# Issue order at the start, layer-1 modulation pieces on VectorE, and a fixed order of adds at both layer ends of a two-layer diffusion trunk

## The chip, the cores and the metric

The kernel runs on one core of a Trainium2 chip. The metric is the device time of one execution in microseconds (us), the median of three runs. Below, PE (TensorE), VectorE (DVE), ScalarE (ACT), GpSimd (POOL) and SyncE (SP) are the engines of that core. Matmul inputs come from on-chip memory (tiles); matmul results land in accumulator banks (PSUM).

## What is computed

Two trunk layers over 512 latent tokens and 256 context tokens, of width 1024, all in fp32. Layer 0 mixes tokens with windowed attention, layer 1 with a chunked gMLP. After each mixer there is a LayerNorm, then a mixture of experts (16 experts, two per token, one router for both layers), then a second LayerNorm. Shift, scale and gate of each step come from a "modulation" product of the conditioning vector.

```
mod = silu(c) @ w_mod[i] + b_mod[i]           # shift, scale, gate; 6 x 1024 per layer
x   = layer_norm(ALPHA * x + g_a * mixer(x * (1 + sc_a) + sh_a))
y   = sum over 2 experts e of gate_e * (silu(h @ w1[e]) * (h @ w3[e])) @ w2[e]
x   = layer_norm(ALPHA * x + g_f * y)         # "layer end" below
# gMLP: z = gelu(h @ w_in + b_in); u, v = halves of z
#       v = layer_norm(v); s = w_s (per group of 128 channels) @ v + b_s; out = (u * s) @ w_out
```

## The kernel before, in words

**Weights as pieces.** All weights stream from HBM as pieces of 128 x 1024 fp32 (512 KB). The list `pieces` (L153 to 185) fixes in which order they are loaded, and `issue` (L194) starts them on the SP queue, each into a tile of the pool `S`, which has 28 tiles (`NS`, L25). That pool is shared with split weights, intermediates and the rows that come back from the experts, so a load waits until a tile is free. `raw`, `hl` and `adv` (L248 to 262) start loads ahead: `LR` and `LS` say how many pieces ahead to load and to split, and inside the experts `LOOK` = 25 does (L1159). `split` (L226) turns a piece into a high and a low part, a ScalarE cast and a VectorE subtraction, for the matrices that go through three matmuls instead of one.

**The start (L266 to 430).** SP loads a block of columns, the first modulation pieces (`mod`), two blocks of constants (`ct`, `cc`), two small rows of 16 numbers (`sinkv`, `rb`) that are broadcast to 128 partitions, and writes zeros to the rows of the HBM array `ydr` that stand for "no result". 16 `mod` pieces go through PE (`gemv`, L336); their result `mcol` modulates the context (`cT`) and the tokens (`xT`) in `hsplit` (L402), which yields a high and a low part on ScalarE and VectorE. With the split `qkv` pieces these feed the first projection (L439 to 441).

**Modulation pieces on vectors.** The other 80 modulation pieces (`mt`; 32 of layer 0, 48 of layer 1) are multiplied by the row silu(c) and summed along the row, in `gemt` (L365): either in one VectorE instruction (L368), or as a GpSimd product (L370) and a ScalarE sum (L371). 64 of them run beside the attention. The last 16 run beside the gMLP, two in each of its 8 steps, odd ones on VectorE, even ones on GpSimd and ScalarE. For these 16 the row silu(c) is loaded again just ahead of the 8 steps (L1402).

**Experts (`moe`, L1126).** Tokens are gathered from HBM into units of 32, 64 or 128 rows. 12 pieces per expert pass through `gemm1` (L1045) and `gemm2` (L1078). Most units write their result to `ydr` by a GpSimd DMA; the last two units stay in PSUM. `collect` (L1111) gathers the two results of each token back from `ydr` with 8 indirect GpSimd DMAs, and `combine` (L1120) adds each to the token's row with one VectorE instruction.

**Layer end (`last_norm`, L681).** The last two units are spread to their tokens by matmuls with a 0/1 matrix (`rows`, L692) into PSUM, VectorE adds that to `X` (`add`, L701), ScalarE sums squares (L710), and VectorE computes 1/sqrt by Newton steps on tiny tiles (`newton`, L737) for two token tiles at a time. In layer 0, `pre` (L1334) then transposes the normalised rows for the gMLP, and GpSimd multiplies and adds the LayerNorm row (L1355, L1356). In layer 1 each tile is normalised on ScalarE (L1439), multiplied (L1440) and added to (L1441) on VectorE, but for the first two tiles whose addition is on GpSimd, and stored.

**gMLP.** `vhalf` (L1359) makes v in 8 steps of 24 matmuls; `vnorm` (L1367) normalises each of the four token tiles; then 8 steps (L1404 to 1429) each make one 128-channel block of u (24 matmuls, L1409 to 1411), mix v (L1419), and multiply on VectorE (L1422, L1425, L1428).

**What sets the order.** The build orders each engine's instructions with a simulated timeline (L1497): of those whose inputs it expects to be there, the one written first goes first, and `high_priority` blocks go ahead. `in_order` (L667) ties the instructions of a block on the named engines to the order in which they are written. Before, `last_norm` uses it for its own additions and norms, while `combine` stands outside it.

Of the kernel before, what the change touches and what calls it, by code (L numbers as in the profile page):

```python
# [18 lines left out]
D = 1024  # L19
# [85 lines left out]
def hybrid_kernel(ctx: ExitStack, tc: tile.TileContext, A, out):  # L105
# [127 lines left out]
    def ensure_split(n):  # L233
        while nsplit[0] < min(n, limit[0]):
            p = pieces[nsplit[0]]
            if p[0] not in KSPLIT:
                if p[0] == "zero":
                    issue(nsplit[0] + 1)
                elif nsplit[0] not in used:
                    return  # L240
            else:
                issue(nsplit[0] + 1)
                pairs[p] = split(raws[p])
            nsplit[0] += 1
# [164 lines left out]
    cT, hT = {}, {}  # L409
    att = ExitStack()  # L410
# [270 lines left out]
    def last_norm(l, X, py, gf):  # L681
# [5 lines left out]
        v = [small([128, 3, 2], F32, "xv") for _ in range(2)]  # L687
        o = [psA(), psA(), psT(), psT()]
        o = [[o[0][:, :512], o[0][:, 512:]], [o[1][:, :512], o[1][:, 512:]], o[2:], [psB(), psB()]]
        ys = slot([128, 512], F32, "ys")  # L690

        def rows(t, u, y):  # L692

            for n in range(2):
                PE.matmul(o[t][n], R["oT"][n * 64:n * 64 + 64, u, t * 128:(t + 1) * 128], y[n * 64:n * 64 + 64, :],
                          start=(u == 0), stop=(u == 1))

        for t in range(4):
            rows(t, 0, R["yp"])
# [13 lines left out]
        def var(t):  # L713
            w = v[t // 2][:, 0, t % 2:t % 2 + 1]
# [3 lines left out]
        def norm(i):  # L718
            var(2 * i)
            var(2 * i + 1)  # L720
            y = newton([v[i][:, k] for k in range(3)], "x", 2)
            nmr = small([128, 2], F32, "xm")
            V.tensor_mul(nmr, nmu[:, 2 * i:2 * i + 2], y)
            return y, nmr

        with in_order(PE, V, SC):
            V.scalar_tensor_tensor(ys, py, R["gs"][:, 1:2], gf, op0=OP.mult, op1=OP.mult)
            for t in range(4):
                rows(t, 1, ys)
            for t in range(4):  # L730
                add(t, 0)
                add(t, 1)
                mean(t)
            r = norm(0), norm(1)
        return r

    def newton(v, w, n=1):  # L737

        y = small([128, n], F32, w + "ny")
# [5 lines left out]
        u = small([128, n], F32, w + "nu")  # L745
# [374 lines left out]
    def combine(l, a, X):  # L1120

        R = RT[l]
        for t in range(4):
            V.scalar_tensor_tensor(X[t], R["y", t, a], R["g"][:, a, t:t + 1], X[t], op0=OP.mult, op1=OP.add)  # L1124

    def moe(l, rest, X):  # L1126
# [25 lines left out]
        def stage(i):  # L1152
# [3 lines left out]
            def adv():  # L1156
                if lastuse:
                    done[0] += 1
                    issue(first + done[0] + LOOK)  # L1159
            return lambda j: raw("moe", l, v, j), adv  # L1160

        def fin():
# [4 lines left out]
            elif i == n - 2:  # L1167
                R["yp"] = slot([128, 512], F32, "ys")
                V.scalar_tensor_tensor(R["yp"], py, R["gs"][:, 0:1], gf[64], op0=OP.mult, op1=OP.mult)
            return py  # L1170

        for i, (v, o, m, row) in enumerate(units):
# [17 lines left out]
            if i == n // 2:  # L1190
                gates()
            if i == n - 4:
# [6 lines left out]
            if i == n - 1:  # L1199
                combine(l, 1, X)  # L1200
            pend = (i, to_hT(m, s))
        py = fin()
        combine(l, 0, X)
# [113 lines left out]
    binv = load_row(A["binv"], alloc=uslot)  # L1317

# [48 lines left out]
    def vnorm(t):  # L1367
        v = vv[t]
        rstd, nmr = ln_stats(v, "c")
        SC.activation(v, v, AF.Identity, bias=nmr, scale=rstd)  # L1370

    for t, (y, nmr) in zip((0, 2), last_norm(0, X, py, gf)):
        for i in range(2):
            SC.activation(X[t + i], X[t + i], AF.Identity, bias=nmr[:, i:i + 1], scale=y[:, i:i + 1])
# [13 lines left out]
    for t in range(4):  # L1388
        vhalf(t, 1)
        vnorm(t)  # L1390
# [11 lines left out]
    srow[0] = load_row(sdr, alloc=uslot)  # L1402
    gated = []
    for f in range(8):  # L1404
# [7 lines left out]
        for j in range(2):  # L1412
            gemt(1, 32 + 2 * f + j)
# [22 lines left out]
    for t, (y, nmr) in zip((0, 2), last_norm(1, X, py, gf)):  # L1436
        for i in range(2):
# [63 lines left out]
```

## Time and profile before

| | |
|---|---|
| three runs, us | 1185.77, 1188.14 (median), 1191.42 |
| the profiled execution, us | 1186.24 |
| its span, first to last instruction | 1184.4 |
| mean granted PE clock | 0.925 |
| busy: PE, VectorE, ScalarE, GpSimd | 1014.6, 611.5, 359.9, 271.2 us |
| DMA | 330.62 MB, mean 279 GB/s |

The span runs through start (to about 86 us), attention (to 290), layer 0's output projection and router (to 380), layer 0's experts (to 647), layer end (to 674), gMLP (to 860, with its output projection and router), layer 1's experts (from 886 to 1147), layer end. Shares are means over these stages, so each stage is read on its own below. "Busy" counts time inside instructions; a PE clock of 1.00 is 2.4 GHz and 0.50 is 1.2 GHz.

### The profile page before, as it was taken

The page shows a single profiled execution, that of the slowest core. Times are in us where ns is not written, and L with a number is a line of the kernel's source. Part 1 is how long each engine was busy: PE and PEld are TensorE (multiplying, and loading weights), DVE is VectorE, ACT ScalarE, POOL GpSimd, SP SyncE. Part 2 cuts the span into 40 slices and gives each one's busy share as a digit, 9 for nine tenths or more (in the row PEclk, how much of TensorE's full clock was granted, in tenths as well). Part 3 has the DMA queues.
Part 4 walks back from the last instruction along what each step waited for, and adds up shares of the span by engine and source line. Part 5 has one row for each costly group of instructions (what it writes and reads, how often), then busy time and mean ns, then how long its engine had stood idle before and what let it go on. Part 6 is the DMA issues. An engine that isn't in the chain of part 4 may idle for free. (4 is left out here: it accounts for less than half of the span.)

```text
span 1184.4 us, 18461 instructions
## 1 busy us (share of the span) xinstructions
PE 1014.6 (86%) x6596; PEld 589.6 (50%) x6596; DVE 611.5 (52%) x1548; ACT 359.9 (30%) x730; POOL 271.2 (23%) x262
## 2 busy tenths in 40 slices
PE   5799899996992999999999399599929999999980
PEld 2577665554782444444443178488713342444420
DVE  1798988785457621221122896876565121221247
ACT  1553487775312111111121343442212110111103
POOL 0044333323000123231213251410001221120131
PEclk7799999998996999999999799799959999999995
DMA  9934457547274999999998316365449999898991
GB/s 346 408 148 174 157 196 258 173 145 256 102 269 160 377 409 390 410 410 409 410 386 324 118 46 244 131 212 203 178 189 387 410 411 410 311 407 352 386 382 71
DMA packets 104284, 330.62 MB, mean 279 GB/s; under 512 B 13346, under 2 KB 24306, under 8 KB 104179
## 3 DMA queue, kind: packets, MB, share of 16 engines
q1 hardware_dynamic: 88608, 287.56, 63.4%
q0 software_dynamic: 10848, 26.75, 6.0%
q10 hardware_dynamic: 4722, 14.98, 3.5%
q8 instruction: 56, 0.92, 0.3%
q14 instruction: 50, 0.40, 0.1%
HBM read 310.72 MB, written 21.67 MB: 281 GB/s over the span
## 5 line engine op out<-in xcount | busy, mean ns | idle before, releaser
L1045 PE MATMUL pb<-ring,xt 128*32 128x256 f32 (+1 forms) x2112 | 228.1, 440 | 1.1 <-DMA ring<-in_moe 0.8
L1045 PEld LDWEIGHTS pb<-ring,xt 128*32 128x32 f32 (+1 forms) x2112 | 86.7, 117 | 114.9 <-issue 70.4
L1089 POOL DMA_DIRECT2D ydr<-ys x132 | 67.0, 513 | 319.2 <-DVE ys L1084 258.9
L1056 DVE TENSOR_TENSOR si<-si,pb 128x128 f32<-128x128 f32 (+1 forms) x46 | 16.1, 350 | 206.9 <-ACT si L1055 203.4
L370 POOL TENSOR_TENSOR raw<-raw,row 128x1024 f32<-128x1024 f32 x32 | 90.8, 2850 | 131.8 <-DMA raw<-in_mt 104.5
L1078 PE MATMUL pb<-ring,hh 128*32 128x256 f32 (+1 forms) x1056 | 119.5, 441 | 1.7 <-ACT hh L1067 0.8
L368 DVE SCALAR_TENSOR_TENSOR raw<-raw,row 128x1024 f32<-128x1024 f32 x48 | 83.6, 1760 | 4.1 <-DMA row<-sdr 4.1
L1055 ACT ACTIVATE si<-pb 128x128 f32<-128x128 f32 (+1 forms) x46 | 15.1, 329 | 219.4 <-PE pb L1045 219.4
L1078 PEld LDWEIGHTS pb<-ring,hh 128*32 128x32 f32 (+1 forms) x1056 | 43.0, 117 | 62.5 <-issue 45.8
L1084 DVE TENSOR_TENSOR ys<-pb,gfs 128x256 f32<-128x256 f32 (+1 forms) x42 | 22.6, 537 | 81.5 <-PE pb L1078 79.9
L1008 POOL DMA_INDIRECT xg<-hdr,Rgi x22 | 23.3, 1057 | 178.6 <-DVE pq L887 87.7
L230 DVE TENSOR_TENSOR wl<-raw,wh 128x1024 fp32r<-128x1024 f32 x44 | 53.8, 1247 | 15.3 <-ACT wh L229 15.2
L1067 ACT COPY hh<-pt 128x128 f32<-128x128 f32 (+2 forms) x50 | 17.0, 339 | 146.1 <-PE pt L1065 139.4
L569 DVE TENSOR_SCALAR_CACHE_REDUCE P<-pa,nsink 128x512 f32<-128x512 f32 (+1 forms) x64 | 50.5, 809 | 19.7 <-PE pa L565 10.9
L1045 PE MATMUL pa<-ring,xt 128*128 128x512 f32 x128 | 59.4, 604 | 0.6 <-DVE xt L1027 0.6
L571 ACT ACTIVATE P<-P,nm 128x512 f32<-128x512 f32 (+1 forms) x64 | 49.5, 775 | 11.9 <-DVE P L569 11.6
L605 ACT COPY PT<-pt 128x512 f32<-128x512 f32 x72 | 39.4, 582 | 27.2 <-PE pt L604 27.0
L604 PE MATMUL pt<-cc,P 128*128 128x128 f32 x288 | 43.9, 281 | 4.1 <-ACT PT L605 3.5
L229 ACT CAST wh<-raw 128x1024 fp32r<-128x1024 f32 x44 | 44.5, 1044 | 8.7 <-DMA mdr<-gr 6.9
L604 PEld LDWEIGHTS pt<-cc,P 128*128 128x128 f32 x288 | 31.0, 141 | 31.0 <-issue 25.2
L1025 ACT ACTIVATE xt<-pt,bc,gc 128x128 f32<-128x128 f32 x88 | 33.1, 457 | 38.2 <-PE pt L1019 20.9
L614 PE MATMUL pb<-PT,Vt 128*64 128x512 f32 x144 | 38.8, 617 | 3.6 <-ACT PT L605 3.6
(368 smaller groups left out, 2005.0 us busy)
## 6 DMA issues: line engine op xcount, KB each, us to landing
ring<-in_moe SPq DMA_DIRECT2D x336, 512.0 KB
raw<-in_mt SPq DMA_DIRECT2D x80, 512.0 KB
raw<-in_moe SPq DMA_DIRECT2D x48, 512.0 KB
raw<-in_mod SPq DMA_DIRECT2D x16, 512.0 KB
raw<-in_qkv SPq DMA_DIRECT2D x12, 512.0 KB
ydr<-zero SPq DMA_DIRECT2D x10, 512.0 KB
ydr<-ys POOLq DMA_DIRECT2D x36, 128.0 KB, 5.6
raw<-in_wo SPq DMA_DIRECT2D x8, 512.0 KB
```

Of the source, the lines that this page charges most:

```text
L229: SC.copy(hi, src)
L230: V.tensor_sub(lo, src, hi.bitcast(F32))
L368: V.scalar_tensor_tensor(w, w, 1.0, srow[0], op0=OP.mult, op1=OP.mult, accum_out=mv[l][:, j:j + 1])
L370: GP.tensor_mul(w, w, srow[0])
L569: V.tensor_scalar(P[j], reg, -0.125, nsink[:, p * 8 + j:p * 8 + j + 1], op0=OP.mult, op1=OP.min, accum_out=nm[:, j:j + 1])
L571: SC.activation(P[j], P[j], AF.Exp, bias=nm[:, j:j + 1], scale=-1.0, accum_out=sums[:, j:j + 1])
L604: PE.transpose(pt[:, j * 128:(j + 1) * 128], P[a * 4 + j][:, i * 128:(i + 1) * 128], idf)
L605: cp = SC.copy(tl[:, a, :], pt)
L614: m.append(PE.matmul(po[a * 64:(a + 1) * 64, :], Vt[kb // 3][:, kb % 3, g * 64:(g + 1) * 64], tl[:, a, :], start=(i == 0), stop=(i == nb - ...
L1045: PE.matmul(o.rearrange("p (m c) -> p m c", m=2), xt[:, k, c:c + n], w[:, h], start=(k == 0), stop=(k == 7), skip_group_check=True)
L1078: PE.matmul(o, ht[f], w[:, h], start=(f == 0), stop=(f == 3), skip_group_check=True)
L1089: GP.dma_start(ydr[row:row + n, h * n * 8:(h + 1) * n * 8], ys[h * n:h * n + n, :])
```

## The change

1. Start: `cc` is loaded after 14 `mod` pieces instead of six; `sinkv` and `rb` are loaded from the ScalarE queue; the zeros of `ydr` that are written at the start go out from the GpSimd queue; the first two `qkv` pieces are loaded and split under `high_priority`, ahead of the context's `hsplit`.
2. Order of pieces: four of the gMLP's `winv` pieces are loaded ahead of the last 16 expert pieces of layer 0, with four pieces more of look-ahead there, and split while the last but one unit runs.
3. gMLP: the row silu(c) is loaded before the layer end. The last 16 `mt` pieces all run on VectorE, are ordered behind the last `vnorm`, and are spread over steps 1 to 7 as 3, 3, 2, 2, 2, 2, 2.
4. Layer ends: the whole of it is written in one fixed order for PE, VectorE and ScalarE. For token tiles 2 and 3 the gathered row `y(t, 0)` is added by PE (a diagonal matrix of gates times the row, fp32) instead of VectorE.
5. Layer 0's end normalises the first two tiles before the fourth tile is summed. Layer 1's end does one Newton pass for all four tiles, replaces ScalarE's normalisation, product and addition by two VectorE instructions per tile, does the second of these for tile 1 on PE (diagonal times row, plus the row b2), with ScalarE copies, and has no GpSimd work.

```diff
-    pieces += moe_pieces(0)
-    pieces += [("winv", j) for j in range(8)] + [("ws",)]
+    first = moe_pieces(0)
+    pieces += first[:-16] + [("winv", j) for j in range(4)] + first[-16:]
+    pieces += [("winv", j) for j in range(4, 8)] + [("ws",)]
+    LATE = [0, 0, 3, 6, 8, 10, 12, 14, 16]
     for j in range(8):
-        pieces += [("winu", j), ("mt", 1, 32 + 2 * j), ("mt", 1, 33 + 2 * j)]
+        pieces += [("winu", j)] + [("mt", 1, 32 + i) for i in range(LATE[j], LATE[j + 1])]
...
-    issue(6)
+    issue(14)
     cc = cst.tile([128, C_KEEP], F32, name="cc")
     SP.dma_start(cc, A["consts"][:, :C_KEEP])
-    issue(10)
-    SP.dma_start(sinkv, A["sink"].to_broadcast([128, 16]))
+    SC.dma_start(sinkv, A["sink"].to_broadcast([128, 16]))
-    SP.dma_start(rb, A["rbias"].to_broadcast([128, 16]))
+    SC.dma_start(rb, A["rbias"].to_broadcast([128, 16]))
...
-        SP.dma_start(ydr[z:z + 1, :].rearrange("o (a b) -> (o a) b", b=128), zero[0:8, :])
+        GP.dma_start(ydr[z:z + 1, :].rearrange("o (a b) -> (o a) b", b=128), zero[0:8, :])
...
-    SP.dma_start(ydr[free:ZR[0], :].rearrange("p (a b) -> p a b", b=128),
+    GP.dma_start(ydr[free:ZR[0], :].rearrange("p (a b) -> p a b", b=128),
...
-    def gemt(l, j):
+    def gemt(l, j, past=None):
         w = raw("mt", l, j)
-        if (j % 4 != 3 if l and j < 32 else j % 2):
-            V.scalar_tensor_tensor(w, w, 1.0, srow[0], op0=OP.mult, op1=OP.mult, accum_out=mv[l][:, j:j + 1])
+        if past or (j % 4 != 3 if l else j % 2):
+            m = V.scalar_tensor_tensor(w, w, 1.0, srow[0], op0=OP.mult, op1=OP.mult, accum_out=mv[l][:, j:j + 1])
+            if past:
+                after(m, past)
...
+    with tc.high_priority():
+        for q in [("qkv", j) for j in range(2)]:
+            issue(pos[q] + 1)
+            pairs[q] = split(raws[q])
...
+        dg = [tt2([128, 128], F32, "dg") for _ in range(2)]
+        for i in range(2):
+            SC.activation(dg[i], idf, AF.Identity, scale=R["g"][:, 0, 2 + i:3 + i])
...
+        def scaled(u, p):
+            V.scalar_tensor_tensor(ys[u], p, R["gs"][:, u:u + 1], gf, op0=OP.mult, op1=OP.mult)
+            for t in range(4):
+                rows(t, u, ys[u])
 
         with in_order(PE, V, SC):
...
+            scaled(0, R["py"])
+            combine(l, 1, X, 0, 2)
+            scaled(1, py)
+            for t in (2, 3):
+                for n in range(2):
+                    PE.matmul(o[t][n], dg[t - 2], R["y", t, 0][:, n * 512:n * 512 + 512], start=False, stop=True)
+            combine(l, 1, X, 2, 4)
+            combine(l, 0, X, 0, 2)
+            finish(X, sums, norm, nmu)
...
-                    issue(first + done[0] + LOOK)
+                    issue(first + done[0] + LOOK + (0 if l or done[0] < 160 else 4))
...
+            if i == n - 2 and not l:
+                for q in [("winv", j) for j in range(4)]:
+                    issue(pos[q] + 1)
+                    pairs[q] = split(raws[q])
...
     binv = load_row(A["binv"], alloc=uslot)
+    srow[0] = load_row(sdr, alloc=uslot)
...
+    def middle(X, sums, norm, nmu):
+        def pair(t):
+            y = norm(t, t + 2)
+            nmr = small([128, 2], F32, "xm")
+            V.tensor_mul(nmr, nmu[:, t:t + 2], y)
+            for i in range(2):
+                SC.activation(X[t + i], X[t + i], AF.Identity, bias=nmr[:, i:i + 1], scale=y[:, i:i + 1])
+        for t in range(3):
+            sums(t)
+        pair(0)
+        sums(3)
+        pair(2)
...
-        for j in range(2):
-            gemt(1, 32 + 2 * f + j)
+        for j in range(LATE[f], LATE[f + 1]):
+            gemt(1, 32 + j, normed)
...
-            x = X[t + i]
-            SC.activation(x, x, AF.Identity, bias=nmr[:, i:i + 1], scale=y[:, i:i + 1])
-            V.tensor_mul(x, x, g2)
-            (GP if t == 0 else V).tensor_add(x, x, b2)
-            SP.dma_start(out[0, (t + i) * 128:(t + i + 1) * 128, :], x)
+        def scaled(t):
+            V.scalar_tensor_tensor(z[t], X[t], nmu[:, t:t + 1], g2, op0=OP.add, op1=OP.mult)
+        def done(t, y):
+            V.scalar_tensor_tensor(z[t], z[t], y[:, t:t + 1], b2, op0=OP.mult, op1=OP.add)
+            SP.dma_start(out[0, t * 128:(t + 1) * 128, :], z[t])
+        for t in range(4):
+            sums(t)
...
+            PE.matmul(p[:, ns], idf, b2[:, ns], start=True, stop=False, skip_group_check=True)
+        scaled(0)
+        scaled(1)
+        y = norm(0, 4)
+        V.tensor_scalar(dg, idf, y[:, 1:2], None, op0=OP.mult)
+            PE.matmul(p[:, ns], dg, z[1][:, ns], start=False, stop=True, skip_group_check=True)
+        done(0, y)
+            SC.copy(o[:, ns], p[:, ns])
+        SP.dma_start(out[0, 128:256, :], o)
+        for t in (2, 3):
+            scaled(t)
+            done(t, y)
```

## Rows read from the trace of the kernel before

**Rows 1.** Waits of PE, 30 to 60 us: instruction, releaser, total us, times, longest.
```profile
PE pb L439 <- ACT wh L229: 5.0, 1, 5.0
```

**Rows 2.** Waits of PE, 640 to 890 us, same columns.
```profile
PE pt L1341 <- ACT x L1374: 17.4, 1, 17.4
PE pt L1419 <- ACT v L1370: 11.7, 1, 11.7
```

**Rows 3.** SP's queue, timeline of the start: start us, us, queue, line, DMA, count.
```profile
10.80 0.33 SPq L281 DMA_DIRECT2D sinkv<-in_sink  x1
...
15.97 6.59 SPq L213 DMA_DIRECT2D raw<-in_mod  x6
```

**Rows 4.** Windows of 2 us: stretch, length, PE, PEld, DVE, ACT, POOL, PEclk, DMA share, GB/s.
```profile
16.00:18.00 2.00, 1.36 (x16) 0.35 (x16) 0.00 (x0) 0.00 (x0) 0.00 (x0) 0.63 1.01 406
18.00:20.00 2.00, 1.71 (x14) 0.58 (x10) 0.69 (x1) 0.59 (x1) 0.00 (x0) 0.50 0.60 162
20.00:22.00 2.00, 2.00 (x16) 1.63 (x15) 0.32 (x2) 0.00 (x0) 0.00 (x0) 0.50 0.72 276
```

**Rows 5.** ScalarE, timeline of the start: start, us, instruction, count, idle before and releaser.
```profile
39.81 1.98 ACT L229 CAST wh<-raw 128x1024 fp32r<-128x1024 f32 x2
```

**Rows 6.** SP's queue and PE, timelines near the end of layer 0's experts.
```profile
624.73 6.77 SPq L213 DMA_DIRECT2D raw<-in_winv  x8
...
632.42 7.09 PE L1045 MATMUL pb<-ring,xt 128*64 128x512 f32 x32
```

**Rows 7.** VectorE, timeline of layer 0's end.
```profile
649.51 2.35 DVE L230 TENSOR_TENSOR wl<-raw,wh 128x1024 fp32r<-128x1024 f32 x2
...
656.48 1.28 DVE L1124 SCALAR_TENSOR_TENSOR x<-y,pg,x 128x1024 f32<-128x1024 f32 x1 [1.56 <-DMA y<-ydr,prow]
659.18 3.79 DVE L1124 SCALAR_TENSOR_TENSOR x<-y,pg,x 128x1024 f32<-128x1024 f32 x3 [1.43 <-DMA y<-ydr,prow]
```

**Rows 8.** VectorE, timeline of the gMLP's first steps.
```profile
737.85 1.23 DVE L368 SCALAR_TENSOR_TENSOR raw<-raw,row 128x1024 f32<-128x1024 f32 x1 [4.11 <-DMA row<-sdr]
...
739.00 3.42 DVE L368 SCALAR_TENSOR_TENSOR raw<-raw,row 128x1024 f32<-128x1024 f32 x1
...
750.27 2.26 DVE L748 SCALAR_TENSOR_TENSOR cnu<-cny,cnv 128x1 f32<-128x1 f32 x1
```

**Rows 9.** Windows of 5 us behind that wait; columns as in rows 4.
```profile
755.00:760.00 5.00, 3.81 (x13) 3.15 (x14) 3.89 (x6) 4.73 (x9) 0.00 (x0) 0.50 0.51 176
760.00:765.00 5.00, 4.96 (x14) 3.49 (x13) 4.83 (x8) 1.90 (x3) 1.03 (x1) 0.60 0.69 220
```

**Rows 10.** VectorE, timeline of two later gMLP steps (first multiply of each).
```profile
780.39 0.75 DVE L1422 SCALAR_TENSOR_TENSOR sg<-pt,cols,bs 128x512 f32<-128x512 f32 x1 [1.13 <-PE pt L1419]
...
787.04 0.74 DVE L1422 SCALAR_TENSOR_TENSOR sg<-pt,cols,bs 128x512 f32<-128x512 f32 x1
```

**Rows 11.** Chain of waits, layer 1's experts and end: start us, us, what.
```profile
1087.08 7.06 PE pa L1078 x16
...
1145.51 1.28 DVE x L1124
...
1158.48 1.23 DVE x L703 x4
...
1161.42 0.13 DVE xv L715
...
1164.43 0.17 DVE xm L723
...
1170.64 2.28 DVE xnu L750
...
1179.15 1.14 DVEq L1497
```

**Rows 12.** GpSimd, timeline of layer 1's end.
```profile
1167.28 5.61 POOL L1441 TENSOR_TENSOR x<-x,row 128x1024 f32<-128x1024 f32 x2 [18.32 <-DVE xnu L751]
```

**Rows 13.** Windows of 5 us, first attention unit; columns as in rows 4.
```profile
145.00:150.00 5.00, 3.76 (x19) 3.21 (x17) 5.00 (x16) 4.63 (x12) 0.00 (x0) 0.50 0.05 14
```

More of the change, by code (lines that the diff above doesn't have):

```diff
@@ L240, in ensure_split @@
                     return
-            else:
+            elif p not in pairs:
                 issue(nsplit[0] + 1)
@@ L679, in in_order, with last_norm @@
                     before[e] = i
-    def last_norm(l, X, py, gf):
+    def last_norm(l, X, py, gf, finish):
         R = RT[l]
@@ L695, in rows @@
                 PE.matmul(o[t][n], R["oT"][n * 64:n * 64 + 64, u, t * 128:(t + 1) * 128], y[n * 64:n * 64 + 64, :],
-                          start=(u == 0), stop=(u == 1))
-        for t in range(4):
-            rows(t, 0, R["yp"])
+                          start=(u == 0), stop=(u == 1 and t < 2))
         def add(t, n):
@@ L713, in var, with norm, sums @@
         def var(t):
-            w = v[t // 2][:, 0, t % 2:t % 2 + 1]
+            w = v[:, 0, t:t + 1]
             V.tensor_scalar(w, q[:, t, 0:1], q[:, t, 1:2], 1.0 / D, op0=OP.add, op1=OP.mult)
             V.tensor_scalar(w, w, EPS, None, op0=OP.add)
[L718 to L724, printed above, removed]
-        with in_order(PE, V, SC):
[L727 to L735, printed above, removed]
+        def norm(a, b):
+            for t in range(a, b):
+                var(t)
+            return newton([v[:, k, a:b] for k in range(3)], "x", b - a)
+        def sums(t):
+            add(t, 0)
+            add(t, 1)
+            mean(t)
+        def scaled(u, p):
+            V.scalar_tensor_tensor(ys[u], p, R["gs"][:, u:u + 1], gf, op0=OP.mult, op1=OP.mult)
+            for t in range(4):
+                rows(t, u, ys[u])
+        with in_order(PE, V, SC):
+            scaled(0, R["py"])
[7 more added lines that the diff above has]
+            finish(X, sums, norm, nmu)
     def newton(v, w, n=1):
-        y = small([128, n], F32, w + "ny")
+        y = small([128, max(n, 4 * (n > 1))], F32, w + "ny")[:, :n]
         yi = y.bitcast(I32)
@@ L744, in newton @@
         V.tensor_scalar(v[2], v[0], 0.0625, None, op0=OP.mult)
-        u = small([128, n], F32, w + "nu")
+        u = small([128, max(n, 4 * (n > 1))], F32, w + "nu")[:, :n]
         for i in range(3):
@@ L1118, in collect, with combine @@
                                   bounds_check=ZR[l], oob_is_err=False)
-    def combine(l, a, X):
+    def combine(l, a, X, t0, t1):
         R = RT[l]
-        for t in range(4):
+        for t in range(t0, t1):
             V.scalar_tensor_tensor(X[t], R["y", t, a], R["g"][:, a, t:t + 1], X[t], op0=OP.mult, op1=OP.add)
@@ L1167, in fin @@
             elif i == n - 2:
[L1168 to L1169 removed]
+                R["py"] = py
             return py
@@ L1369, in vnorm @@
         rstd, nmr = ln_stats(v, "c")
[L1370 to L1374, printed above, removed]
+        return SC.activation(v, v, AF.Identity, bias=nmr, scale=rstd)
+    def middle(X, sums, norm, nmu):
[10 more added lines that the diff above has]
+        pair(2)
+    last_norm(0, X, py, gf, middle)
     with in_order(V, SC):
@@ L1389, in hybrid_kernel @@
         vhalf(t, 1)
-        vnorm(t)
+        normed = vnorm(t)
     bsr = load_row(A["bs"], alloc=uslot)
@@ L1433, in hybrid_kernel, with end @@
     b2 = load_row(A["ln2_b"][1:2, :])
-    for t, (y, nmr) in zip((0, 2), last_norm(1, X, py, gf)):
-        for i in range(2):
-            x = X[t + i]
-            SC.activation(x, x, AF.Identity, bias=nmr[:, i:i + 1], scale=y[:, i:i + 1])
-            V.tensor_mul(x, x, g2)
-            (GP if t == 0 else V).tensor_add(x, x, b2)
-            SP.dma_start(out[0, (t + i) * 128:(t + i + 1) * 128, :], x)
+    def end(X, sums, norm, nmu):
+        z = [slot([128, D], F32, "z") for _ in range(4)]
+        o = slot([128, D], F32, "z")
+        dg = tt2([128, 128], F32, "dg")
+        def scaled(t):
[5 more added lines that the diff above has]
+            sums(t)
+        p = psA()
+        halves = [slice(n * 512, n * 512 + 512) for n in range(2)]
+        for ns in halves:
+            PE.matmul(p[:, ns], idf, b2[:, ns], start=True, stop=False, skip_group_check=True)
[3 more added lines that the diff above has]
+        V.tensor_scalar(dg, idf, y[:, 1:2], None, op0=OP.mult)
+        for ns in halves:
+            PE.matmul(p[:, ns], dg, z[1][:, ns], start=False, stop=True, skip_group_check=True)
+        done(0, y)
+        for ns in halves:
+            SC.copy(o[:, ns], p[:, ns])
[3 more added lines that the diff above has]
+            done(t, y)
+    last_norm(1, X, py, gf, end)
 def host_arrays(inputs):
```

8 lines of the change are left out of this document (2 added, 6 removed).

## The prediction

> **What bounds the kernel now.** I began with the windows of equal length. In the two expert stages and in most of the gMLP PE is busy without a break, so a change gains only where PE stands still. The waits of PE say where that is. Three places lie in the reach of this change: 5.0 us before the first projection matmul, released by a ScalarE cast [rows 1]; 17.4 us at layer 0's end, until the first normalised tile can be transposed; and 11.7 us in the gMLP, until the last v tile is normalised [rows 2]. The fourth is layer 1's end, which no wait of PE shows as PE is done by then; the chain of waits shows it, one VectorE instruction after another from 1145.51 to 1180.3 (1179.15 plus 1.14) [rows 11]. The span of 1184.4 ends 4.1 us later, with the last store. All sums are made against the profiled execution, 1186.24 us; the median of the three runs stands 1.9 us above it.
>
> **Start: -2.0.** SP issues four small transfers between 10.80 and the next weight piece at 15.97, so for 5.2 us it starts no weights [rows 3]. Some 8 us later the DMA engines run dry: from 18 to 22 us they move 162 and 276 GB/s where 406 were reached before [rows 4]. The loss is 2 x (1 - 162/406) + 2 x (1 - 276/406) = 1.8 us. Everything up to the projection follows the arrival of weights, so moving these issues should give 1.8 back. The Trainium skill, "DMA: Bandwidth & Descriptors", section "Issuing engines are not separate DMA queues", speaks against such a move: all queues end on the same sixteen engines, and another issuer saves only the issuing time. The rows agree in so far as the engines' own share fell too, to 0.60 and 0.72 [rows 4]; by the rule only that idle share comes back, 2 x 0.40 + 2 x 0.28 = 1.4 us.
>
> The two `qkv` casts that move ahead take 1.98 us for both [rows 5]. They go into time in which ScalarE waits for weights, so PE's wait of 5.0 can shrink, but VectorE still has to make every low part before the projection can end. I count 0.2 for them. The other end is that the whole 5.0 goes. What is moved also costs: two issues on ScalarE and three on GpSimd, both idle then; and `cc` behind eight more weight pieces, 8 x 524 KB / 406 GB/s = 10.3 us later. The last weight pieces before the projection cover that, unless VectorE's order puts the casts from `cc` ahead of the modulation work; then the 1.8 is lost again. Bounds: -5.0 to +1.8.
>
> **Expert pieces of layer 0: 0.** Four `winv` pieces ahead of the last 16 expert pieces delay those by 4 x 524 / 406 = 5.2 us. The last expert load had been issued by 624.73, when the `winv` loads begin, and the last expert's first matmul starts at 632.42, eight pieces taking 7.09 us [rows 6]. So the loads lead PE by more than that delay, and the lead hides it. Without this cover it costs 5.2. The eight splits run beside these matmuls, on engines that have nothing else to do.
>
> **Layer 0's end: -6.3.** Off VectorE's path to the first normalised tile go: four `winv` subtractions, two of which take 2.35, so 4.7 [rows 7]; two `combine` of 1.28, done by PE, so 2.6 [rows 7]; and the sum of the fourth token tile, 1.23 for its two additions [rows 11] and some 0.2 for its mean, so 1.4. That is 8.7. But VectorE already stood still twice for gathered rows, 1.56 and 1.43, until 659.18 [rows 7]. The subtractions lie ahead of that, so if the rows come no earlier, only 2.6 + 1.4 = 4.0 are gained and the rest becomes a longer wait. Bounds -4.0 and -8.7. I take the middle, -6.3, since the gathers are issued in the same stretch and VectorE's work delays them in part. PE pays four fp32 matmuls of 512 columns; eight such took 7.06 [rows 11], so 3.5 us, at a time when it waits anyway. They also need the last gathered rows, so these are late next. The GpSimd products of `pre` stay as they were.
>
> **gMLP: -14.5.** Behind PE's 11.7 stands VectorE [rows 8]: it waited 4.11 for the row silu(c), then ran three modulation products, of which the first took 1.23 and the next, beside a GpSimd product, 3.42, and only then the Newton steps of the last v tile, where single tiny operations took 2.26 while GpSimd ran its own products. The change takes all of this out of the way: the row comes before the layer end, the products stand behind the normalisation, and GpSimd has none. So the 11.7 go. Behind the wait PE runs at half clock: granted 0.50 and 0.60, with 3.81 and 4.96 us busy [rows 9]. At full clock that work needs 1.9 and 3.0, so 1.9 + 2.0 = 3.9 come back, and the 1.2 us that PE was not busy from 755 to 760. Together 16.8. Against it: eight products more on VectorE at 1.23, 9.8 us. One step takes 787.04 - 780.39 = 6.65 with PE busy throughout [rows 10]. VectorE needs in it a split subtraction of 1.2 [rows 7], three operations of at most 0.75 [rows 10] and two products of 1.3 with their read-out: 6.1. With three products, in two of the steps, it is 7.4. So VectorE falls behind by 0.8 twice and must catch up at 0.5 a step; I take off 2.3 for that and for a first load that comes late, and keep 14.5. Bounds: -17, and -9.5 by the first rival.
>
> **Layer 1's end: -7.5.** I lay out the new order. VectorE starts with the first gathered row at 1145.51, as before [rows 11]. Six `combine` of 1.28 and one scaling of 0.75 end at 1153.9; four sums of 1.4 end at 1159.5; two products with the LayerNorm row, at 1.28 each as nearest form, at 1162.1; one Newton pass, 1161.42 to 1164.60 before [rows 11], so 3.2, and 0.7 for two more tiles' variances, at 1166.0; the diagonal, 0.2; then five operations of 1.28 at 1172.6. With the store's 4.1 the span ends at 1176.7 instead of 1184.4, 7.7 less. What goes is above all the second Newton pass, whose tiny operations took 2.28 [rows 11] beside 5.61 us of GpSimd additions [rows 12], and a pass over each tile. PE's diagonal product for tile 1 and ScalarE's copies run beside the last five operations. If PE is at half clock, its four 512-column matmuls in the two places take up to 7 us each instead of 3.5 and can come last: -5. If gathered rows come sooner, -9. I take -7.5.
>
> **Sum.** -2.0 - 6.3 - 14.5 - 7.5 = -30.3, so 1155.9 on the profiled execution and 1157.8 on the median. I forecast 1157.
>
> **Rivals.** *VectorE becomes the gMLP's bound* (0.15). The Trainium skill, "Perfetto Trace Analysis", section "Optimizing Scalar/DVE Operations", says that with a saturated VectorE it may pay to hand work to ScalarE or even GpSimd, which is the opposite of this edit; it adds that those two share a port, so it may not help. In rows: the step's 6.1 becomes 7.4 wherever loads bunch, so 7 steps x 0.75 = 5 us are lost, the gain is 9.5, and the time 1162. Against it: 6.1 is under 6.65. *The layer ends wait for gathered rows* (0.15): -4.0 and -5.0 there instead of -13.8 together, 1162. For it: the two waits for these rows [rows 7]. *The start does not move* (0.10), since a rebuilt order holds VectorE there for `cc`: 0, so 1159; this is also what remains if the change doesn't do there what it says. *The attention comes out worse* (0.05): the build orders every engine anew, and nothing in the diff holds the order there, where VectorE is full. In one stretch of it VectorE was busy 5.00 of 5 us, PE 3.76 at clock 0.50 [rows 13]: 1.9 us of full-clock work, so 3.1 lost. 10 such stretches more, 50 of some 200 us, eat the whole gain; from 12 on the kernel is slower, and with 14 it takes 1157 + 43 = 1200. Against it: nothing that feeds the attention changes but its start, by 2 us. The forecast as it stands has the remaining 0.55.
>
> **Numbers.** All bounds on the good side (-5.0, -8.7, -17, -9) give 1147 on the profiled execution; all on the bad side (+1.8, -4.0, -9.5, -5.0) give 1170. Neither will come together; the upper end is stretched a little for milder cases of the last rival. Range 1147 to 1172. A difference of 0.5%, 6 us, is about what a measurement of this kernel can tell from none; all cases but the last are far beyond it. Faster 0.95, within it 0.02, slower 0.03.
>
> **What would show it.** Right: DMA above 380 GB/s throughout 18 to 22 us; PE's wait before the first transposes under 12 us; no wait of PE for the last v tile and clock 1.00 through the eight gMLP steps, each near 6.5; all L368 products there near 1.23; last VectorE operation about 27 us after the first gathered row, 35 before. Wrong: a PE wait of over 5 us anywhere in the gMLP, a wait for expert pieces before 645, or PE waits in the attention longer than before by over 10 us.

## The result, and the profile after

The changed kernel takes 1172.0 us (median of four runs, 1169.9 to 1175.6); the kernel before, on the same chip, 1188.9. The ratio is 0.986, 95% interval 0.983 to 0.990. It is faster, as forecast, but by 16 to 17 us and not by 30; 1172 is the upper end of the range given. The profiled execution of the changed kernel is its slowest, 1175.6 us, span 1173.8.

Two of the places predicted look as they should. In the windows of 2 us the gap of [rows 4] is gone and the clock is full:

```profile
16.00:18.00 2.00, 2.00 (x18) 1.53 (x22) 0.17 (x1) 0.00 (x0) 0.00 (x0) 1.00 1.01 404
18.00:20.00 2.00, 2.00 (x24) 0.91 (x20) 0.00 (x0) 0.05 (x1) 0.00 (x0) 1.00 1.04 416
20.00:22.00 2.00, 2.00 (x19) 0.66 (x11) 0.69 (x1) 0.53 (x1) 0.00 (x0) 1.00 1.01 404
```

In the gMLP, PE's waits from 738 to 800 us hold nothing of the 11.7 of [rows 2], and the sixteen products on VectorE, of which the first and the last stand here from its timeline, all take 1.22 or 1.23 us where [rows 8] had 3.42:

```profile
PE pb L1436 <- ACT wh L231: 1.7, 1, 1.7
PE pb L1438 <- DVE wl L232: 0.5, 1, 0.5
PE pt L1446 <- DVE sg L1449: 0.2, 1, 0.2
```
```profile
745.98 1.23 DVE L369 SCALAR_TENSOR_TENSOR raw<-raw,row 128x1024 f32<-128x1024 f32 x1
...
785.08 1.22 DVE L369 SCALAR_TENSOR_TENSOR raw<-raw,row 128x1024 f32<-128x1024 f32 x1
```

Where the rest went is read from one view, the instructions of a line with the start of their first and last: the projection's matmuls with `hTh`, the score matmuls, the v projection with `gh`, the products of the gMLP steps with the low part of the weights. Before, then after:

```profile
L439 PE MATMUL pb<-wh,hTh x96: 392/396/628, 55.3 to 137.7; 128*128 128x512 f32 x96
L558 PE MATMUL pa<-kT,qT x64: 274/420/583, 138.4 to 277.9; 128*128 128x256 f32 x32, 128*128 128x384 f32 x32
L439 PE MATMUL pb<-wh,gh x64: 387/389/795, 676.9 to 728.4; 128*128 128x512 f32 x64
L1411 PE MATMUL pb<-gh,wl x64: 388/389/797, 731.3 to 798.3; 128*128 128x512 f32 x64
```
```profile
L446 PE MATMUL pb<-wh,hTh x96: 389/396/796, 53.0 to 143.4; 128*128 128x512 f32 x96
L565 PE MATMUL pa<-kT,qT x64: 275/420/582, 144.1 to 284.9; 128*128 128x256 f32 x32, 128*128 128x384 f32 x32
L446 PE MATMUL pb<-wh,gh x64: 387/389/777, 681.1 to 738.6; 128*128 128x512 f32 x64
L1438 PE MATMUL pb<-gh,wl x64: 388/389/632, 741.5 to 795.8; 128*128 128x512 f32 x64
```

The eight steps take 54.3 us for 67.0. But the projection begins 2.3 earlier and ends 5.7 later, and the v projection takes 57.5 for 51.5. PE's waits of the changed kernel, from 60 to 140 us, then 655 to 682, then 682 to 740, say what it stood for:

```profile
PE pt L497 <- DVE kl L491: 5.0, 1, 5.0
PE pb L446 <- DVE rp L462: 2.2, 1, 2.2
...
PE pt L1358 <- ACT x L1395: 5.3, 1, 5.3
...
PE pb L448 <- DVE gl L1371: 4.3, 7, 0.9
```

The second is what is left of the 17.4 of [rows 2], well under the 12 forecast. The first and the third are new or grown, and both lead to VectorE instructions beside a GpSimd product. The kernel before has, from 60 to 140 and from 670 to 730 us:

```profile
PE pt L490 <- DVE kl L484: 3.0, 2, 1.6
...
PE pb L441 <- DVE gl L1354: 2.2, 3, 0.9
```

For the third, see the changed kernel's VectorE timeline and, below it, GpSimd's:

```profile
687.29 0.15 DVE L768 SCALAR_TENSOR_TENSOR xny<-xnu,xny 128x2 f32<-128x2 f32 x1
687.36 1.36 DVE L1366 TENSOR_SCALAR ht<-pt,gc,bc 128x128 f32<-128x128 f32 x4
688.64 1.41 DVE L766 TENSOR_TENSOR xnu<-xny 128x2 f32<-128x2 f32 x1
689.97 0.41 DVE L1371 TENSOR_TENSOR gl<-ht,gh 128x256 fp32r<-128x256 f32 x1
690.30 2.33 DVE L767 TENSOR_TENSOR xnu<-xnu,xv 128x2 f32<-128x2 f32 x1
692.56 0.41 DVE L1371 TENSOR_TENSOR gl<-ht,gh 128x256 fp32r<-128x256 f32 x1
```
```profile
687.63 2.40 POOL L1372 TENSOR_TENSOR x<-x,row 128x1024 f32<-128x1024 f32 x1 [3.00 <-ACT gh L1370]
690.11 2.51 POOL L1373 TENSOR_TENSOR x<-x,row 128x1024 f32<-128x1024 f32 x1
```

Two Newton operations on 128x2 values, which take 0.16 us elsewhere, last until GpSimd's instruction ends, at 690.03 and 692.62. The four `ht` operations, which read PSUM, pass beside it at 0.34 each. The Trainium skill, "SBUF — State Buffer", section "🔬 SBUF: two separate sides", states it so: whichever of the two engines, VectorE and GpSimd, starts first has the shared ports for the whole instruction, and VectorE needs them in certain modes or with two SBUF inputs. The trace agrees for these operations, which have two inputs each.

In the kernel before, the last steps of the second Newton stood beside such a product too, as its VectorE timeline shows:

```profile
677.00 2.01 DVE L751 TENSOR_TENSOR xnu<-xnu,xv 128x2 f32<-128x2 f32 x1
...
679.26 2.33 DVE L752 SCALAR_TENSOR_TENSOR xny<-xnu,xny 128x2 f32<-128x2 f32 x1
```

The change put nearly the whole of it there: its result `xm` came 35.8 us after the experts' end (E in the table below) before, and 41.4 after.

The end of layer 1, from VectorE's timeline (the first combination with a gathered row, the last operation on z):

```profile
1141.48 1.28 DVE L1140 SCALAR_TENSOR_TENSOR x<-y,pg,x 128x1024 f32<-128x1024 f32 x1 [4.42 <-DMA y<-ydr,prow]
...
1167.54 1.28 DVE L1472 SCALAR_TENSOR_TENSOR z<-z,xny,row 128x1024 f32<-128x1024 f32 x1
```

### The profile page after: what moved, and what is told of

Read it like the earlier page. It is cut to its first block, busy times and chain, and to the rows that moved or that the text cites. A ratio compares the mean times of both kernels' runs of the same rounds, so it can differ in the third digit from the quotient of the medians.

```text
span 1173.8 us, 18480 instructions
## 1 busy us (share of the span) xinstructions
PE 1036.0 (88%) x6620; PEld 596.0 (51%) x6620; DVE 608.9 (52%) x1546; ACT 348.9 (30%) x716; POOL 240.9 (21%) x255
## 5 line engine op out<-in xcount | busy, mean ns | idle before, releaser
L369 DVE SCALAR_TENSOR_TENSOR raw<-raw,row 128x1024 f32<-128x1024 f32 x56 | 91.8, 1659 | 0.0
L373 POOL TENSOR_TENSOR raw<-raw,row 128x1024 f32<-128x1024 f32 x24 | 69.2, 2896 | 96.3 <-DMA raw<-in_mt 96.2
L578 ACT ACTIVATE P<-P,nm 128x512 f32<-128x512 f32 (+1 forms) x64 | 49.5, 775 | 13.0 <-DVE P L576 12.7
## 6 DMA issues: line engine op xcount, KB each, us to landing
ring<-in_moe SPq DMA_DIRECT2D x336, 512.0 KB, 10.7
```

Source lines behind the costliest of these rows:

```text
L369: m = V.scalar_tensor_tensor(w, w, 1.0, srow[0], op0=OP.mult, op1=OP.mult, accum_out=mv[l][:, j:j + 1])
L578: SC.activation(P[j], P[j], AF.Exp, bias=nm[:, j:j + 1], scale=-1.0, accum_out=sums[:, j:j + 1])
```

## The experiments

Single executions of one stage spread by 2 us and more, so stages are compared over all runs. The table gives times of the profiled executions, in us: first and last projection product with `hTh`; last score product; end of layer 0's experts (first product of the last experts' rows, called E); from E to the first transpose; the v projection; from E to the first low-part product of the gMLP steps (the middle); the steps, from there to the last such product; the span.

| run | first | last | score | E | E to transposes | v | middle | steps | span |
|---|---|---|---|---|---|---|---|---|---|
| before | 55.3 | 137.7 | 277.9 | 647.4 | 27.1 | 51.5 | 83.9 | 67.0 | 1184.4 |
| b_gmlp | 56.1 | 139.1 | 280.7 | 651.7 | 28.5 | 51.5 | 85.3 | 52.7 | 1173.9 |
| a_nostart | 54.6 | 137.0 | 279.3 | 651.4 | 23.9 | 57.2 | 86.9 | 54.3 | 1169.1 |
| c_nostart | 54.1 | 138.6 | 279.9 | 651.1 | 19.5 | 49.9 | 76.0 | 54.3 | 1160.0 |
| a_noprio | 52.9 | 135.3 | 280.2 | 650.5 | 23.1 | 57.6 | 87.0 | 54.3 | 1168.7 |
| a_nomoves | 53.8 | 139.0 | 279.0 | 649.9 | 24.4 | 57.5 | 87.7 | 54.0 | 1169.5 |
| after | 53.0 | 143.4 | 284.9 | 654.6 | 23.0 | 57.5 | 86.9 | 54.3 | 1173.8 |
| a_mid | 53.1 | 139.1 | 283.7 | 651.8 | 25.4 | 53.1 | 83.8 | 54.3 | 1167.7 |
| b_norm4 | 52.8 | 138.8 | 284.0 | 654.3 | 26.2 | 49.9 | 82.7 | 52.7 | 1167.1 |
| b_gplate | 52.8 | 139.7 | 284.2 | 652.7 | 23.3 | 53.5 | 83.0 | 54.3 | 1167.4 |
| b_rows | 52.9 | 143.3 | 286.3 | 654.5 | 19.9 | 50.7 | 77.2 | 54.3 | 1163.9 |
| c_gprows | 53.1 | 142.3 | 285.6 | 655.6 | 16.7 | 53.6 | 76.6 | 54.3 | 1164.2 |
| c_v0 | 52.9 | 134.3 | 272.9 | 643.1 | 19.9 | 50.0 | 76.4 | 55.6 | 1153.0 |
| c_v0nostart | 54.4 | 136.4 | 275.4 | 648.5 | 21.9 | 50.2 | 78.7 | 54.1 | 1159.3 |

**The start undone, whole and by halves.** Three runs from the changed kernel.

```diff
 a_nostart and a_nomoves
-    issue(14)
+    issue(6)
     SP.dma_start(cc, ...)
+    issue(10)
     ...
-    SC.dma_start(sinkv, ...)        # rb the same; the two fills of ydr from GP to SP
+    SP.dma_start(sinkv, ...)
...
 a_nostart and a_noprio
-    with tc.high_priority():
-        for q in [("qkv", j) for j in range(2)]:
...
```

a_nostart: 

> The changed kernel with all edits at the start undone (small loads, constants and zero fills back on SP's queue between the weights, the first two qkv splits without priority). Theory: the edits at the start cost the projection stage more than they brought, since they move GpSimd's 128x1024 products onto the VectorE chain of the k and v units. Then the first product with hT is at 55.3 us and the last projection product at about 137.7 as in the kernel before (53.0 and 143.4 in the changed one), and the time is some 5.7 us under the changed kernel's, near 1168. Rival: the projection stage lost its 8 us to something outside these edits, or to a spread between executions; then the last projection product is still at 143 to 146 and the time is 1174 to 1178.

a_noprio: 

> The changed kernel without the priority of the first two qkv splits, the queue moves kept. If the priority is what upset the projection stage, the last projection product is near 137 us and the time near 1168. If the queue moves did it, the last projection product stays near 143 and the time near 1174, and the first product with cT is later than 37.1 us by up to 2.

a_nomoves: 

> The changed kernel with the queue moves undone and the priority kept. If the queue moves upset the projection stage, its last product is near 137 to 139 us and the time near 1168; if the priority did it, it stays at 143 to 146. In both cases the first product with cT is later than 37.1, at 39 to 41.

Measured against the kernel before: 0.987 (0.983 to 0.992), 0.990 (0.986 to 0.994) and 0.988 (0.983 to 0.992), medians 1171.2, 1173.7 and 1170.6 us: no total differs from the changed kernel's by more than the runs spread, so the totals decide nothing (a_nostart's was expected near 1168 by the theory, at 1174 or more by its rival). The stages do differ. The projection starts at 52.8 to 53.1 in the seven kernels with both edits and at 54.1 to 56.1 in the five without. The first product with `cT` came at 38.9 in a_noprio and 37.2 in a_nomoves; the 39 to 41 expected of the latter did not come. Without the edits, or with half of them, the last projection product came at 135.3 to 139.0, near the theory's 137 to 138; but a_mid, whose instructions stand up to there in the order of the changed kernel, had 139.1. So part of the 143.4 is the spread of one execution. Over all runs of the study the last score product separates cleanly: 283.7 to 286.3 in the six kernels with both edits (and GpSimd's products as they were), 277.9 to 280.7 in the four without, 280.2 and 279.0 with half. Means at E: 653.9 and 650.4. In these profiled executions the start edits bring the projection 2 us forward and the experts' end 3.5 us back; no total confirms the 3.5.

**The order of the middle.** Three variants: sums first (a_mid), one Newton (b_norm4), GpSimd held back (b_gplate).

```diff
 a_mid
-        for t in range(3):
+        for t in range(4):
             sums(t)
         pair(0)
-        sums(3)
         pair(2)
...
 b_norm4, behind the four sums, for both pairs
+        y = norm(0, 4)
+        nmr = small([128, 4], F32, "xm")
+        V.tensor_mul(nmr, nmu, y)
+        for t in range(4):
+            SC.activation(X[t], X[t], AF.Identity, bias=nmr[:, t:t + 1], scale=y[:, t:t + 1])
...
 b_gplate, order of the middle kept; both products out of pre(t)
-        pre(3)
+        f = pre(3)
+        for x in X:
+            together(GP.tensor_mul(x, x, lg2), f)
+            GP.tensor_add(x, x, lb2)
```

a_mid: 

> The changed kernel with sums(3) put in front of pair(0), so that both Newton iterations of the middle could follow each other. Theory: the 7 us that the first gMLP stage lost (last v product 738.6 for 728.4 before, its stage begun 4.2 later) come from the second Newton standing among VectorE's instructions of pre(0) and pre(1), under GpSimd's products, where instructions of 0.15 us took 2.3. With sums(3) earlier the second Newton starts 1.5 us earlier, before GpSimd's first product: xm of tiles 2 and 3 comes near 680 us and not at 696, PE's wait of 5.3 us for x at the transposes goes, and the time is 4 to 7 us lower, near 1170. Rival: the products of GpSimd hurt pre itself, whatever the order of the Newtons; then the time stays within 1.5 us of the changed kernel's. Its first 640 us are the changed kernel's, so they also show whether the last projection product at 143.4 repeats (to 1 us) or was the spread of one execution.

b_norm4: 

> The changed kernel with one fixed order in the middle: sums of all four tiles, then one Newton iteration over four columns in place of two over two. From the end of layer 0's experts (first product with the last two experts' rows) to the first product of the eight gMLP steps the kernel before took 83.9 us, the changed one 86.9, and the variant that only put sums(3) in front of pair(0) 83.8; in that one two small instructions of the second Newton still took 2.0 and 2.3 us beside GpSimd's product. Theory (the second Newton under GpSimd's products holds the transposes): no Newton is left there, xm of all tiles comes by 677 to 678, PE's wait for x at the transposes is that of tile 0 alone, and the stretch is 79 to 82 us. Rival (GpSimd's products slow pre's own VectorE instructions, whatever the Newtons do): the stretch stays at 83 to 85. The instructions up to the end of layer 0's experts are the changed kernel's, so the last projection product is a repeat: 143.4 and 139.1 us so far.

b_gplate: 

> The changed kernel with its order of the middle kept, but GpSimd's eight 128x1024 products of x held until the last VectorE instruction of pre(3). Theory: nothing then stands beside the second Newton, its instructions take 0.15 to 0.2 us, xm of tiles 2 and 3 comes by 684 (696.0 in the changed kernel), and the stretch from the experts' end to the gMLP steps falls from 86.9 to about 81 us. Rival (the second Newton is late by its place behind sums(3), not by GpSimd): xm still comes after 690 and the stretch stays over 85.

Medians 1170.9, 1169.1 and 1169.1 us (0.988, 0.983 to 0.993; 0.987, 0.983 to 0.990; 0.987, 0.984 to 0.991): each within 3 us of the changed kernel, so the stage decides. The middle takes 86.9 to 87.7 in the four kernels that keep it as changed, and 83.8, 82.7 and 83.0 here: some 4 us back. In a_mid `xm` of tiles 2 and 3 came at 685.9, not near 680, since two of its operations were still held; PE's wait for x, which is tile 0's, did not go but was 6.8, so that sentence of the expectation misread it. In b_norm4 it came at 678.9 for all tiles and the v projection fell to 49.9, but the first transpose had to wait for all four sums, 26.2 after E for 23.0; that gave half back, and 82.7 is just outside the 79 to 82 expected. In b_gplate every operation of the second Newton took 0.16 us or less, yet `xm` came only at 687.5, as these stand one by one between `pre`'s instructions. So place and GpSimd both delayed it; neither theory had it alone.

**Row loads behind the gathers.**

```diff
+    R["got"] = GP.indirect_dma_start(...)                  # in collect
...
-    binv = load_row(A["binv"], alloc=uslot)                # also sdr, lg2, lb2, bsr
+    late = dict(alloc=uslot, q=GP, past=RT[0]["got"])      # order behind the last gather, no wait
+    binv = load_row(A["binv"], **late)
```

b_rows: 

> The kernel with one Newton over four columns (the run beside this one), and the five row loads of 512 KB (binv, sdr, ln2's two, bs) issued from GpSimd's queue behind the eight gathers, not from ScalarE's beside them. From 648 to 664 us the DMA engines move 314 to 416 GB/s, 2.62 MB of it these rows. Theory (layer 0's end waits for gathered rows because the DMA engines are full): without the rows the last gather lands about 2.62 MB / 400 GB/s = 6.5 us earlier, VectorE's waits for y (9.2 us in sum) fall under 4, and the first transposes come 3 to 6 us earlier relative to the experts' end (23.0 to 25.4 so far). Rival (the gathers are bound by their own 4.19 MB and their descriptors on GpSimd's queue): the gathered rows land as before, the transposes at 23 to 26, and the time within 1 us of the run beside it.

1163.1 us against 1169.1 beside it (0.979, 0.976 to 0.983). VectorE's waits from 640 to 670 us, first b_norm4, then b_rows:

```profile
DVE x L1140 <- DMA y<-ydr,prow: 8.4, 5, 4.1
DVE ys L737 <- PE pb L1094: 3.1, 1, 3.1
```
```profile
DVE ys L739 <- PE pb L1096: 3.1, 1, 3.1
...
DVE x L1142 <- DMA y<-ydr,prow: 2.3, 3, 1.1
```

The waits for gathered rows fall by 6.1, the transposes come 6.3 earlier after E (19.9 for 26.2), the median is 6.0 lower. The DMA engines are as full as before; only the order has changed. From 656 to 664 us, b_norm4, then b_rows:

```profile
656.00:660.00 4.00, 2.04 (x8) 0.57 (x4) 1.58 (x2) 0.00 (x0) 2.42 (x3) 0.98 1.01 356
660.00:664.00 4.00, 3.57 (x10) 1.62 (x12) 1.66 (x2) 0.00 (x0) 0.00 (x0) 0.59 1.02 413
```
```profile
656.00:660.00 4.00, 4.00 (x22) 1.94 (x20) 3.53 (x5) 0.00 (x0) 3.39 (x5) 1.00 0.99 391
660.00:664.00 4.00, 3.10 (x12) 1.15 (x9) 3.96 (x8) 0.00 (x0) 1.82 (x4) 1.00 0.99 389
```

PE's clock, 0.59 where it had stood for the rows, stays at 1.00.

c_gprows puts these loads under the changed kernel's own order of the middle, with GpSimd held back as in b_gplate.

c_gprows: 

> The changed kernel with its own order of the middle (three sums, a pair, the fourth, a pair), GpSimd's products of x held until pre(3) is done, and the row loads behind the gathers. Theory (the two causes, GpSimd's products beside the second Newton and the row loads beside the gathers, are separate and add): the transposes come 17 to 18 us after the experts' end (23.3 with the products held alone, 19.9 with the rows behind the gathers and one Newton), the stretch to the gMLP steps is 76 to 78 us (83.0 and 77.2), and the time is 1162 to 1165. Rival (the early transposes only wait for something else, tile 3's rows or the winv splits): the stretch is over 79.

16.7, 76.6 and 1164.5 us (0.980, 0.976 to 0.985): stage and time as expected, the transposes 0.3 sooner. The two causes are separate and add within the spread. It is no faster than b_rows: the transposes come 3.2 us sooner, and the v projection takes 2.9 longer.

**The gMLP part alone**, in the kernel before.

```diff
-        pieces += [("winu", j), ("mt", 1, 32 + 2 * j), ("mt", 1, 33 + 2 * j)]
+        pieces += [("winu", j)] + [("mt", 1, 32 + i) for i in range(LATE[j], LATE[j + 1])]
...
-            gemt(1, 32 + 2 * f + j)
+            gemt(1, 32 + j, normed)      # on VectorE, behind the last v tile's normalisation
...
+    srow[0] = load_row(sdr, alloc=uslot) # early, behind binv
```

b_gmlp: 

> The kernel before with the gMLP part of the change alone (its pieces' place in the order of the loads, all on VectorE behind the last v tile's normalisation, sdr's row loaded early). Theory: this part carries 12.7 us of the change's gain by itself: the eight gMLP steps from first to last product take 54.3 us for 67.0, the stretch ahead of them keeps the 83.9 of the kernel before, and the time is 12 to 14 us under the kernel before's, about 1174. Rival: it needs the earlier tiles of the middle; then the steps take over 58 us. Its instructions up to the end of the experts are those of the kernel before: a third look at the last projection product (137.7 and 137.0 so far).

1176.5 us, 10.6 under the kernel before (0.992, 0.989 to 0.995), a little less than the 12 to 14 expected. The steps take 52.7 for 67.0. The middle takes 85.3 and not the 83.9 expected; the row load that this part puts there may cost that, as such loads do in b_rows, but no run shows it.

**GpSimd's products of layer 0 on VectorE**, on top of b_rows; and c_nostart and c_v0nostart, which undo the start's edits in b_rows and in c_v0.

```diff
-        if past or (j % 4 != 3 if l else j % 2):
+        if past or not l or j % 4 != 3:      # VectorE; else GpSimd and a sum on ScalarE
```

c_v0: 

> The fastest kernel so far (one Newton over four columns, row loads behind the gathers, 1163.06 us), with all products of layer 0's modulation pieces on VectorE, which in the changed kernel are on GpSimd for every second piece (1.23 us each where VectorE has nothing beside it, against 2.4 us on GpSimd, which hold VectorE up, and a ScalarE sum of 1.05). From the first product with hT to the last projection product VectorE was busy 82 to 88 us in the ten kernels looked at, some 61 of it by the durations that its instructions have alone; 14 or 15 GpSimd products lay beside them. Theory (the edits at the start brought nothing because GpSimd's products fall on the k and v units' VectorE instructions: PE's wait of 5.0 us for kl stood in all five kernels with both edits): that wait goes, the last projection product comes at 133 to 137 (138.8 to 143.4 with GpSimd's products), and the time is 3 to 8 us lower. Rival (VectorE is the bound by its own work there and eight more products of 1.23 us add to it): the last projection product stays at 139 or later and the time does not fall.

c_nostart: 

> The fastest kernel so far with all edits at the start undone. With both edits the last score product of the attention came at 283.7 to 286.3 us in five kernels, without them at 277.9 to 280.7 in three, with one of the two at 279.0 and 280.2. Theory (the edits at the start cost 3 to 5 us by the end of the attention): last score product at 278 to 281, time 1158 to 1161. Rival (what is lost there is made up by the wait for layer 0's routing or experts): last score product early, time within 1.5 us of 1163.

c_v0nostart: 

> Layer 0's products on VectorE, one Newton, rows behind the gathers, and the edits at the start undone. If GpSimd's products are why the edits at the start bring nothing, then without these products the edits are worth their 2 to 4 us: this kernel is 2 to 4 us slower than the one of this call that keeps the edits (first product with cT at 40 to 42 for 37.1, last projection product later by as much). Rival: the edits cost time by another way than GpSimd, and this kernel is the faster one.

c_v0 takes 1152.1 us (0.970, 0.966 to 0.974), 11 under b_rows and 20 under the changed kernel: the fastest of the study. PE's longest wait from 60 to 140 us, and its matmuls by line:

```profile
PE pt L499 <- DVE kl L493: 1.9, 1, 1.9
```
```profile
L448 PE MATMUL pb<-wh,hTh x96: 392/396/796, 52.9 to 134.3; 128*128 128x512 f32 x96
L567 PE MATMUL pa<-kT,qT x64: 280/420/583, 121.7 to 272.9; 128*128 128x256 f32 x32, 128*128 128x384 f32 x32
```

The wait of 5.0 for `kl` is 1.9, and the projection ends 9.0 us before that of b_rows (4.5 before the earliest of the six). From the first to the last projection product, b_rows and then c_v0 (stretch, length, PE, PEld, DVE, ACT, POOL, clock, DMA share, GB/s):

```profile
52.90:143.30 90.40, 80.17 (x383) 64.22 (x384) 78.32 (x111) 34.96 (x70) 37.52 (x15) 0.94 0.47 172
```
```profile
52.90:134.30 81.40, 78.98 (x387) 64.06 (x388) 67.65 (x133) 25.09 (x50) 0.00 (x0) 0.96 0.52 193
```

VectorE does 22 instructions more and is busy 10.7 us less. The gain is above the 3 to 8 expected, and the last score product comes 13.4 earlier than in b_rows (10.8 to 13.4 than in the six). Two more things differ in this kernel, and no run takes them apart: ScalarE's sums are gone (25.1 us busy for 35.0), and the build starts the score products before the projection ends, at 121.7. The second alone is not the cause: a_nomoves, with GpSimd's products, starts them at 125.8, and its last came at 279.0.

c_nostart takes 1162.2 us (0.979, 0.974 to 0.984) against b_rows's 1163.1: within the spread, though its profiled execution is 6.4 us ahead at the last score product and 3.9 at the end. Here the rival's number was met and the theory's stage, so the total doesn't decide. c_v0nostart takes 1158.6 (0.975, 0.971 to 0.979), 6.5 more than c_v0 where 2 to 4 were expected; the two intervals just overlap. Its profiled execution is 1.5 behind c_v0 at the first projection product, 2.5 at the last score product, 5.4 at E, 6.3 at the end; what lies behind the 2.5 has no cause shown. So without GpSimd's products the start's edits seem to pay. Read the other way, taking these products off GpSimd brings 11 us where the start is edited, and only 3.6 where it is not (c_nostart to c_v0nostart, intervals overlapping; last score product 4.5 earlier).

## Why the prediction was wrong

The sum was -30.3. By the table and the end of layer 1 the change made -14.3: +3.5 at the start (means at E), +3.0 in the middle, -12.7 in the gMLP steps, -0.4 from there to the last expert product, -7.7 behind it; the ratio says -16.4. (The two profiled executions alone differ by 7.2 at E, and so by 10.6 in all.) Of the 16.0 us that are missing, 9.3 lie at layer 0's end, 5.5 up to E and 1.8 in the gMLP.

- **"Start: -2.0"** fell, and the wrong premise is "Everything up to the projection follows the arrival of weights", followed only up to the projection's first product. DMA does run through, and over all runs the projection starts 2.0 earlier, as forecast. Behind it VectorE sets the pace: of the changed kernel's 10.3 us of PE's waits from 60 to 140 us, 8.3 are for VectorE's tiles (5.0 `kl`, 2.2 `rp`, 1.1 `qT`). In the kernels with GpSimd's products, the durations of VectorE's instructions from the first to the last projection product add up to 82 to 88 us (they overlap at their ends; it was busy 75 to 79), where the shortest durations of their kind (1.22 a product, 1.21 a split's subtraction, 0.68 a `kl`) add up to some 61. Beside them lay 14 or 15 GpSimd products. There the edits turned into a wait of 4.9 or 5.0 for `kl`, in all six kernels that have both; the others have 2.3 to 3.8. Some of VectorE's instructions under the products, from its timeline, and GpSimd's:

```profile
78.17 4.55 DVE L232 TENSOR_TENSOR wl<-raw,wh 128x1024 fp32r<-128x1024 f32 x2
...
88.49 2.82 DVE L491 TENSOR_TENSOR kl<-rp,kh 128x512 fp32r<-128x512 f32 x1
```
```profile
78.36 12.40 POOL L373 TENSOR_TENSOR raw<-raw,row 128x1024 f32<-128x1024 f32 x4 [14.56 <-DMA raw<-in_mt]
```

  Shown, in profiled executions: with both edits the attention ends 5 us later; without GpSimd's products the loss is gone. Not shown: that the time suffers (0.987 with the start undone for 0.986, and 0.979 for 0.979 in b_rows's pair). Argued only: how much of it is the earlier start and how much the few neighbouring VectorE instructions that the build swapped there. That the start "does not move" was nearest among the rivals; "the attention comes out worse" named the engine, VectorE, but put it down to a new order.
- **"Expert pieces of layer 0: 0"** held: from the last score product to E 369.7 us, before 369.5.
- **"Layer 0's end: -6.3"** fell twice. First, "the gathers are issued in the same stretch and VectorE's work delays them": the last row that VectorE waited for came no earlier after E (11.5 us for 11.8), as the lower bound and a rival said, so the first transpose came 23.0 after E for 27.1, -4.1. The cause was in sight and not counted: the five row loads, one of them new there, share the DMA engines with the gathers, and cost 6.0 us (b_rows). Second, "The GpSimd products of `pre` stay as they were" is true of the products, but now nearly the whole of the second Newton stands beside them, where before its last steps did. The v projection takes 57.5 for 51.5, and 49.9 once that Newton is out of it (b_norm4). With the products held back and the rows behind the gathers (c_gprows), the middle is 76.6, 7.3 under the kernel before: the -6.3 was there to be had.
- **"gMLP: -14.5"** was right in mechanism and 1.8 too large. A step has PE busy for 6.65 [rows 10], so eight need 53.2 (b_gmlp and b_norm4 have 52.7), and no more than some 14 of the 67.0 could go; my 16.8 added clock and wait beyond that. The first rival, VectorE as the bound there, did not come.
- **"Layer 1's end: -7.5"** was right in mechanism and size: -7.7 behind the start of the last expert product (41.1 before, 33.4 after). From the first gathered row at 1141.48 to 1168.82, VectorE's part takes 27.3, for 27.1 forecast and 34.8 before. The rest are two small differences that nearly cancel: the first row came 1.1 after that product's start for 2.2, and the store took 5.0 for 4.1. The rival that saw rows delay both layer ends was right in layer 0 alone.

## What to carry to other kernels

An edit that starts a stage earlier is worth what the stage's own limit leaves of it: read what bounds the stage up to its last instruction, not its first. When a chain of small VectorE operations is moved, look at what GpSimd runs at its new place; and where VectorE has little time free, a product "given" to GpSimd can cost more than doing it. Loads that nobody waits for yet belong behind the gathers that somebody does wait for.

## Not expected of the hardware

Putting GpSimd's products of layer 0 on VectorE made VectorE's own stage shorter: its 61 us of work had been stretched by a third or more. And one order of instructions gives stage ends that differ by up to 4.6 us between executions (last projection product 138.8 to 143.4 with both start edits), while the middle repeats to 1 us.
